# A hybrid pool/SSD layer: the transposed copies of x and B come from VectorE blocks and a trip through DRAM

## The chip, the cores and the metric

The kernel runs on one core of a Trainium2 chip. The metric is the device time of one execution in microseconds (us). Three executions were timed. One further execution was profiled; every row below is from it.

## What is computed

One layer of a streaming encoder on 384 tokens (256 of a prompt, 8 streams with 16 tokens each), model width 2048, everything in float32. The part that matters here is branch B, a Mamba-2 scan with 8 groups of 8 heads:

```python
proj = u @ w_in                       # columns: pool | z | xBC | dt | gates
xbc  = silu(causal_conv(proj[xBC]))   # x: 4096 columns, B: 1024, C: 1024
# per chunk and group g, heads r of the group:
cb  = einsum('btgn,bsgn->btsg', C, B)
xdt = x * dt
y   = einsum('btgr,bsgrp->btgrp', cb * decay, xdt) + einsum('btgn,bgrpn->btgrp', C, h) * exp(cum)
h   = h * exp(last) + einsum('bsgn,bsgr,bsgrp->bgrpn', B, w_end, xdt)
```

A projection leaves its columns (channels) on the partitions and the tokens along the row. The products with `xdt`, and those that make the new state out of B and x, need the tokens on the partitions. So of each group four tiles of x and one tile of B, each 128 channels x 384 tokens, are wanted transposed as well: 40 tiles in all.

## The kernel before

**Matmuls.** Weights and activations are split into a high and a low part in fp32r (`wsplit`, lines 66-72: ScalarE copies the high part, VectorE subtracts to get the low one), and each product is three matmuls (`mm3`, lines 97-100). A projection (`proj`, line 126) is two halves (`half`, line 106) of 8 x 3 matmuls; each half uses one weight tile of 512 KB, fetched by a DMA issued from the SP queue (`wfetch`, line 61). There are three buffers for fetched tiles and three for each split part. `take` (line 117) keeps three weight tiles in preparation: it issues the fetch and the split of the tile two halves ahead before the half itself.

**The scan stage** (lines 549-933) goes through 8 groups. A group projects 10 column tiles, that is 20 halves: B, C, x0, x1, x2, x3, then z0 to z3. After each x, B or C projection `conv_in` and `taps` (lines 565-593) evict it, run the convolution on VectorE and ScalarE and end with the SiLU that writes the tile `xs`.

Between projections stand short runs of small matmuls, called lumps here. One lies in the middle of the group, after x2's projection, and one at its end. The lump in the middle serves the second pair of heads of the group before and the first pair of this group; the one at the end serves the first and the second pair of this group. A lump holds, in this order, `t_pp` (new prompt state), `t_trx` (the transpositions of a pair's two x tiles on TensorE, three 128x128 blocks each, into PSUM), in the middle lump also `t_cb` (C times B) and `t_trB` (the transposition of B), then `t_yT`, `t_Y`, `t_yi`, and `t_su` (state of the streams).

`xside` (line 716) multiplies the transposed x out of PSUM by two per-token factors into `xdt` and `xdw`, splits `xdw` into `xhl`, and sends the last 128 tokens of it to DRAM and back in another order (`x_scr`, then 8 loads into `xst`). `bside` (line 688) splits the transposed B into `Bhl` and does the same (`b_scr`, then 8 loads into `bst`). `xhl` and `Bhl` go into `t_pp`, `xst` and `bst` into `t_su`, `xdt` into `t_Y`.

**Order.** A planner orders each engine's instructions, and the SP queue's DMAs, by program order and by when its own model says that they can start. TensorE is tied further: `chain` and `last` put each half and each lump behind the one before. An engine, and the SP queue, then works strictly in that order: what waits holds up what stands behind it.

Of the kernel before, what the change touches and what calls it, by code (L numbers as in the profile page):

```python
# [14 lines left out]
P = 128  # L15
# [18 lines left out]
def build(ctx, tc, io):  # L34
# [82 lines left out]
    def take(src, name):  # L117
# [5 lines left out]
        assert got == name, (got, name)  # L123
        return hl

    def proj(units, rhs, name):
        o = bank[0](f"pj_{name}")[:, :T]
        for q, src in enumerate(units):
            half(o, q, take(src, f"{name}_{q}"), rhs)
        return o  # L130

    def moving(o, units, lhs, tail, done, pool=None, own=0, hook=None, mid=None):
# [65 lines left out]
    gb_scr = [dram.tile([P, 3, 512], F32, name=f"gb_scr{i}") for i in range(4)]  # L198
    b_scr = [dram.tile([P, 2, P], F32, name=f"b_scr{i}") for i in range(G)]
    x_scr = [dram.tile([P, 2, 2, P], F32, name=f"x_scr{i}") for i in range(16)]  # L200
    cum_scr = dram.tile([NH, T], F32, name="cum_scr")
    dec_scr = dram.tile([NH, NB], F32, name="dec_scr")

# [345 lines left out]
    with tc.tile_pool(name="phd", bufs=2, reuse_waits="tile") as pd, tc.tile_pool(  # L549
# [45 lines left out]
        def conv(ui, c, tag, nb):  # L595
            return taps(conv_in(ui, c), c, tag, nb)

        def lump(fn):
            with behind(last[0]):
                last[0] = fn()  # L600
# [12 lines left out]
                sy.dma_start(cbc, cum_scr[S.h0 + q * 2 : S.h0 + q * 2 + 2, :].partition_broadcast(P))  # L613
                S.cbcs.append(cbc)

        def t_trB(D):
            D.tr = sstile(f"trB{D.g}")
            for b in range(3):
                i = te.transpose(D.tr[:, b * P : b * P + P], D.BT[:, b * P : b * P + P], ident)
            return i  # L620

        def t_cb(D):
            D.cb = sstile(f"cb{D.g}")
            for sb, t0, c0, n in ((0, 0, 0, 256), (1, P, 256, P), (2, TP, T, P)):
                i = te.matmul(
                    D.cb[:, c0 : c0 + n], D.BT[:, sb * P : sb * P + P], D.CT[:, t0 : t0 + n], start=True, stop=True
                )
            return i

        def t_trx(S):  # L630
            S.trs = []
            for j in S.js:
                tr = sstile(f"trx{S.g}_{j}")
                for b in range(3):
                    i = te.transpose(tr[:, b * P : b * P + P], S.D.xs[j][:, b * P : b * P + P], ident)
                S.trs.append(tr[:, :T].rearrange("p (b h q) -> p b h q", b=3, h=2))
            return i

        def t_yi(S):
# [46 lines left out]
            return i  # L686

        def bside(D):
            D.Bhl = pd.tile([P, 2, 3, P], F32R, tag="Bhl", name=f"Bhl{D.g}")
# [4 lines left out]
            sy.dma_start(bscr, D.Bhl[:, :, 2, :].bitcast(F32))  # L694
            D.bs = bst[D.g % 2]
            for p4 in range(4):
                for h2 in range(2):
                    sy.dma_start(
                        D.bs[h2 * 64 + p4 * 16 : h2 * 64 + p4 * 16 + 16].bitcast(F32),
                        bscr.rearrange("(q h r) l n -> h l r q n", q=4, h=2)[h2, p4 // 2],  # L700
                    )

        def cside(D):
            D.Cm = pd.tile([P, 2, P], F32, tag="Cm", name=f"Cm{D.g}", bufs=1)
# [10 lines left out]

        def xside(S):
            S.xdt = pd.tile([P, 2, 3, P], F32, tag="xdt", name=f"xdt{S.nm}")
            S.xdw = pd.tile([P, 2, 3, P], F32, tag="xdw", name=f"xdw{S.nm}", bufs=1)
# [15 lines left out]
            S.xhl = pd.tile([P, 2, 2, 3, P], F32R, tag="xhl", name=f"xhl{S.nm}", bufs=1)  # L734
            s.activation(S.xhl[:, 0], S.xdw, AF.Copy)
            v.tensor_tensor(S.xhl[:, 1], S.xdw, S.xhl[:, 0].bitcast(F32), ALU.subtract)
            xscr = x_scr[S.qd]
            for l in range(2):
                sy.dma_start(xscr[:, l], S.xhl[:, l, :, 2, :].bitcast(F32))
            S.xst = pd.tile([P, 4, 2 * P], F32R, tag="xst", name=f"xst{S.nm}", bufs=1)  # L740
            for p4 in range(4):
                for h2 in range(2):
                    sy.dma_start(
                        S.xst[h2 * 64 + p4 * 16 : h2 * 64 + p4 * 16 + 16].bitcast(F32),
                        xscr.rearrange("(q h r) l j n -> h l r q (j n)", q=4, h=2)[h2, p4 % 2],
                    )

        def eside(S, q):
            if q == 0:
# [99 lines left out]
        for g in range(G + 1):  # L849
            if g == G:  # L850
                eside(prev.p[1], 0)
                eside(prev.p[1], 1)
                dside(prev.p[1])
                gate_b(0, pd, "hs")
                py = mmtile("pp_last")
                lump(lambda: t_pp(prev.p[1], py))
                lump(lambda: t_yT(prev.p[1]))
                lump(lambda: t_Y(prev.p[1]))
                state(prev.p[1])
                final(prev.p[1])  # L860
# [8 lines left out]
            D.BT = conv(u0, 32 + g, "BT", 2)  # L869
            pload(D.p[0])  # L870
            if g:
                eside(prev.p[1], 0)
            D.CT = conv(u0 + 1, 40 + g, "CT", 2)
            if g:
                eside(prev.p[1], 1)
            D.xs.append(conv(u0 + 2, g * 4, "xs", 6))
            if g:
                dside(prev.p[1])
            cload(D.p[0])
            cside(D)  # L880
            D.xs.append(conv(u0 + 3, g * 4 + 1, "xs", 6))
# [48 lines left out]
            state(S)  # L930
            final(S)
            prev = D
# [519 lines left out]
```

## Time and profile before

| | |
|---|---|
| median of 3 executions | 2655.25 us (2655.15 to 2655.45) |
| profiled execution, its own time | 2655.5 us |
| span of its instructions | 2653.7 us |
| TensorE (PE) busy | 2641.6 us |
| VectorE (DVE) busy | 1507.7 us |
| ScalarE (ACT) busy | 1168.8 us |
| the 8 groups of the scan stage | from about 419 to 1131 us of the span |
| one group | about 90 us |

How to read the rows: PE is TensorE's matmuls and PEld its weight loads, SPq the queue of the DMAs that SyncE issues, L70 is line 70 of the kernel, and `wh_x<-w_x` is a tile written and the tile read. "x8" counts instructions. A row of a timeline or of the chain begins with its start and its duration in us, and in brackets stands how long the engine was idle before it and what ended that. A row of the waits tells who waited for whom, us in total, how often, and the longest. Matmuls are pipelined, so the time from one start to the next is what counts.

### The profile page before, as it was taken

To read this page: it belongs to the slowest core of one execution; us is meant where nothing else is said; L and a number is where in the kernel's file an instruction comes from. 1 tells how busy PE (TensorE), PEld (TensorE's weight loads), DVE (VectorE), ACT (ScalarE), POOL (GpSimd) and SP (SyncE) were. 2 spreads that over 40 slices of the span, in tenths; PEclk is the share of its full clock that TensorE was granted. 3 is DMA by queue.
4 is the path that set the end of the run, shared out by engine and by line. 5 is a ranking of instruction groups with operands and counts; after the bars stand their busy time and mean duration, and the time that the engine had idled before them with its cause. 6 is when DMAs were issued, how large, how long until landed. Compare 5 with 4: busy or idle time off the path is not lost.

```text
span 2653.7 us, 38432 instructions
## 1 busy us (share of the span) xinstructions
PE 2641.6 (100%) x15269; PEld 2462.2 (93%) x15269; DVE 1507.7 (57%) x2108; ACT 1168.8 (44%) x1820; POOL 134.5 (5%) x166
## 2 busy tenths in 40 slices
PE   9999999999999999999999999999999999999998
PEld 8998889999999999988888889999999999989897
DVE  6585335788787879856343336534444444444446
ACT  6443225557575756545322235433333333333233
POOL 0000000011111111120000000000000000000000
PEclk9999999999999999999999999999999999999999
DMA  7444445556666666657444543433333343334433
GB/s 273 153 133 156 147 147 205 199 200 218 210 230 210 213 211 223 221 201 254 171 151 163 188 160 132 143 135 135 135 135 135 135 137 135 136 135 135 138 136 129
DMA packets 146163, 451.35 MB, mean 170 GB/s; under 512 B 17920, under 2 KB 45120, under 8 KB 140992
## 3 DMA queue, kind: packets, MB, share of 16 engines
q1 hardware_dynamic: 134400, 389.90, 43.0%
q0 software_dynamic: 11584, 59.00, 6.0%
q8 instruction: 120, 1.97, 0.3%
q14 instruction: 59, 0.48, 0.1%
HBM read 407.11 MB, written 41.72 MB: 169 GB/s over the span
## 4 chain that ended last, share of the span: by engine, by line
PE 97%; ACT 1%; DVE 1%; DMA 1%; issue 0%; SPq 0%; DVEq 0%; ACTq 0%
PE pj_up L98 6%; PE pj_up L100 6%; PE pj_up L99 6%; PE wd L143 6%; PE wd L142 6%; PE wd L141 6%; PE pj_x L98 4%; PE pj_x L99 4%; PE pj_x L100 4%; PE pj_z L100 3%; PE pj_z L99 3%; PE pj_z L98 3%; PE pj_sp L142 3%; PE pj_sp L141 3%; PE pj_sp L143 3%; PE pj_gb L141 2%
## 5 line engine op out<-in xcount | busy, mean ns | idle before, releaser
L98 PE MATMUL pj_up<-x1h,wh_up 128*128 128x384 f32 (+1 forms) x1024 | 333.7, 326 | 0.0
L99 PE MATMUL pj_up<-x1l,wh_up 128*128 128x384 f32 (+1 forms) x1024 | 333.4, 326 | 0.0
L100 PE MATMUL pj_up<-x1h,wl_up 128*128 128x384 f32 (+1 forms) x1024 | 333.4, 326 | 0.0
L71 DVE TENSOR_TENSOR wl_wd<-w_wd,wh_wd 128x1024 fp32r<-128x1024 f32 x126 | 154.3, 1225 | 240.8 <-ACT wh_wd L70 240.8
L141 PE MATMUL wd<-wh_wd,hh 128*128 128x512 f32 x756 | 286.5, 379 | 0.0
L142 PE MATMUL wd<-wl_wd,hh 128*128 128x512 f32 x756 | 286.5, 379 | 0.0
L143 PE MATMUL wd<-wh_wd,hl 128*128 128x512 f32 x756 | 286.5, 379 | 0.0
L70 ACT ACTIVATE wh_wd<-w_wd 128x1024 fp32r<-128x1024 f32 x126 | 133.1, 1057 | 322.6 <-PE wd L143 262.1
L70 ACT ACTIVATE wh_up<-w_up 128x1024 fp32r<-128x1024 f32 x126 | 133.1, 1056 | 292.0 <-PE pj_up L99 231.8
L71 DVE TENSOR_TENSOR wl_up<-w_up,wh_up 128x1024 fp32r<-128x1024 f32 x126 | 154.3, 1225 | 178.1 <-ACT wh_up L70 178.0
L98 PE MATMUL pj_x<-xgh,wh_x 128*128 128x384 f32 x768 | 251.9, 328 | 0.1
L100 PE MATMUL pj_x<-xgh,wl_x 128*128 128x384 f32 x768 | 250.4, 326 | 0.0
L99 PE MATMUL pj_x<-xgl,wh_x 128*128 128x384 f32 x768 | 250.4, 326 | 0.0
L99 PEld LDWEIGHTS pj_up<-x1l,wh_up 128*128 128x128 f32 x1024 | 193.6, 189 | 0.2
L98 PEld LDWEIGHTS pj_up<-x1h,wh_up 128*128 128x128 f32 x1024 | 193.6, 189 | 0.2
L100 PEld LDWEIGHTS pj_up<-x1h,wl_up 128*128 128x128 f32 x1024 | 193.6, 189 | 0.0
L98 PE MATMUL pj_z<-xgh,wh_z 128*128 128x384 f32 x512 | 166.9, 326 | 0.0
L99 PE MATMUL pj_z<-xgl,wh_z 128*128 128x384 f32 x512 | 166.9, 326 | 0.0
L100 PE MATMUL pj_z<-xgh,wl_z 128*128 128x384 f32 x512 | 166.9, 326 | 0.0
L71 DVE TENSOR_TENSOR wl_sp<-w_sp,wh_sp 128x1024 fp32r<-128x1024 f32 x64 | 78.4, 1224 | 154.0 <-ACT wh_sp L70 154.0
L143 PEld LDWEIGHTS wd<-wh_wd,hl 128*128 128x128 f32 x756 | 142.9, 189 | 20.3
L142 PEld LDWEIGHTS wd<-wl_wd,hh 128*128 128x128 f32 x756 | 142.9, 189 | 20.1
(333 smaller groups left out, 5880.6 us busy)
## 6 DMA issues: line engine op xcount, KB each, us to landing
w_up<-w_up SPq DMA_DIRECT2D x128, 512.0 KB, 3.2
w_wd<-w_down SPq DMA_DIRECT2D x128, 512.0 KB, 3.2
w_x<-w_in SPq DMA_DIRECT2D x96, 512.0 KB, 3.6
w_z<-w_in SPq DMA_DIRECT2D x64, 512.0 KB, 3.4
w_sp<-w_ssd SPq DMA_DIRECT2D x64, 512.0 KB, 3.2
w_ga<-w_ga SPq DMA_DIRECT2D x32, 512.0 KB, 3.2
w_pp<-w_pp SPq DMA_DIRECT2D x32, 512.0 KB, 3.2
hs<-ssm POOLq DMA_DIRECT2D x16, 1024.0 KB, 7.0
```

Of the source, the lines that this page charges most:

```text
L70: cut[0] = s.activation(h, w, AF.Copy)
L71: cut[1] = v.tensor_tensor(l, w, h.bitcast(F32), ALU.subtract)
L98: te.matmul(out, wh, xh, start=first, stop=False, **how)
L99: te.matmul(out, wh, xl, start=False, stop=False, **how)
L100: return te.matmul(out, wl, xh, start=False, stop=last, **how)
L141: te.matmul(out, mh, vh, start=k == 0, stop=False)
L142: te.matmul(out, mh, vl, start=False, stop=False)
L143: last[0] = te.matmul(out, ml, vh, start=False, stop=k == nk - 1)
```

## The change

- The 96 transpositions of x (`t_trx`) and the 24 of B (`t_trB`) on TensorE are gone.
- In their place each of the 40 tiles takes a trip, `turned`: VectorE transposes it in 32x32 blocks (`v.transpose`, 128x384, SBUF to SBUF); four DMAs, one for 32 partitions each, write the blocks to their places in a DRAM tile `t_scr` in runs of 32 elements (128 bytes, 384 runs per DMA); one DMA reads it back in rows of 512 bytes with the tokens on the partitions.
- The trip's steps (`turn`, `spread`, read) are put on a list; `tick`, after each half of a projection, lets every listed trip go one step. The old DMA trips of `bside` and `xside` (out, and back) are put on the same list instead of being issued on the spot.
- The projections of a group go x0, x1, B, C, x2, x3 in place of B, C, x0, x1, x2, x3; the columns of the weights follow.
- `xdw` is no tile of its own any more: the second product is written over the transposed x, `xT`. The block-transposed tile `xb` shares its two buffers with the convolution's accumulator, `cacc`.
- In the last group, where no projection follows, `gate_b` calls `tick` at two of its weight tiles.

```diff
+    def tick():
+        for todo in steps:
+            todo.pop(0)()
+        steps[:] = [todo for todo in steps if todo]
     def proj(units, rhs, name):
         for q, src in enumerate(units):
             half(o, q, take(src, f"{name}_{q}"), rhs)
+            tick()
...
+    t_scr = [dram.tile([T, P], F32, name=f"t_scr{i}") for i in range(40)]
...
+        def turned(src, i, o):
+            xb, scr = [], t_scr[i]
+            def turn():
+                xb.append(pd.tile([P, T], F32, tag="cacc", name=f"xb{i}"))
+                v.transpose(xb[0], src)
+            def spread():
+                for q in range(4):
+                    p32 = slice(q * 32, q * 32 + 32)
+                    sy.dma_start(
+                        scr[:, p32].rearrange("(j a) b -> a j b", a=32),
+                        xb[0][p32].rearrange("p (j b) -> p j b", b=32),
+                    )
+            steps.append([turn, spread, lambda: sy.dma_start(o, scr.rearrange("(b t) n -> t b n", b=3))])
+        def xturned(D, g, j):
+            S = D.p[j // 2]
+            if j % 2 == 0:
+                S.xT = pd.tile([P, 2, 3, P], F32, tag="xT", name=f"xT{S.nm}", bufs=1)
+            turned(D.xs[j], g * 4 + j, S.xT[:, j % 2])
...
-        def t_trB(D):
-            D.tr = sstile(f"trB{D.g}")
-            for b in range(3):
-                i = te.transpose(D.tr[:, b * P : b * P + P], D.BT[:, b * P : b * P + P], ident)
...
-        def t_trx(S):
-            for j in S.js:
-                tr = sstile(f"trx{S.g}_{j}")
-                for b in range(3):
-                    i = te.transpose(tr[:, b * P : b * P + P], S.D.xs[j][:, b * P : b * P + P], ident)
...
         def bside(D):
-            s.activation(bh, D.tr[:, :T], AF.Copy)
-            v.tensor_tensor(bl, D.tr[:, :T], bh.bitcast(F32), ALU.subtract)
+            s.activation(bh, bl.bitcast(F32), AF.Copy)
+            v.tensor_tensor(bl, bl.bitcast(F32), bh.bitcast(F32), ALU.subtract)
...
+            steps.append([lambda: sy.dma_start(bscr, D.Bhl[:, :, 2, :].bitcast(F32)), back])
...
         def xside(S):
-            for q, tv in enumerate(S.trs):
-                for o, i in ((S.xdt, 3), (S.xdw, 6)):
+            for q in range(2):
+                tv = S.xT[:, q].rearrange("p b (h q) -> p b h q", h=2)
+                for o, i in ((S.xdt, 3), (S.xT, 6)):
...
-            s.activation(S.xhl[:, 0], S.xdw, AF.Copy)
+            s.activation(S.xhl[:, 0], S.xT, AF.Copy)
...
+            steps.append([out, back])
...
-            cs = [32 + g, 40 + g] + [g * 4 + j for j in range(4)]
+            cs = [g * 4, g * 4 + 1, 32 + g, 40 + g, g * 4 + 2, g * 4 + 3]
...
-                gate_b(0, pd, "hs")
+                gate_b(0, pd, "hs", {0: tick, 2: tick})
...
-            lump(lambda: t_trx(S))
             lump(lambda: t_cb(D))
-            lump(lambda: t_trB(D))
...
             D.xs.append(taps(b2, g * 4 + 2, "xs", 6))
+            xturned(D, g, 2)
             D.xs.append(conv(u0 + 5, g * 4 + 3, "xs", 6))
+            xturned(D, g, 3)
...
-            lump(lambda: t_trx(S1))
```

More of the change, by code (lines that the diff above doesn't have):

```diff
@@ L124, in take @@
         return hl
+    steps = []
+    def tick():
+        for todo in steps:
+            todo.pop(0)()
+        steps[:] = [todo for todo in steps if todo]
     def proj(units, rhs, name):
@@ L614, in cload @@
                 S.cbcs.append(cbc)
-        def t_trB(D):
-            D.tr = sstile(f"trB{D.g}")
-            for b in range(3):
-                i = te.transpose(D.tr[:, b * P : b * P + P], D.BT[:, b * P : b * P + P], ident)
-            return i
         def t_cb(D):
@@ L627, in t_cb @@
                 )
-            return i
-        def t_trx(S):
-            S.trs = []
-            for j in S.js:
-                tr = sstile(f"trx{S.g}_{j}")
-                for b in range(3):
-                    i = te.transpose(tr[:, b * P : b * P + P], S.D.xs[j][:, b * P : b * P + P], ident)
-                S.trs.append(tr[:, :T].rearrange("p (b h q) -> p b h q", b=3, h=2))
             return i
@@ L688, in bside, with back @@
         def bside(D):
-            D.Bhl = pd.tile([P, 2, 3, P], F32R, tag="Bhl", name=f"Bhl{D.g}")
             bh, bl = (D.Bhl[:, a].rearrange("p b n -> p (b n)") for a in range(2))
-            s.activation(bh, D.tr[:, :T], AF.Copy)
-            v.tensor_tensor(bl, D.tr[:, :T], bh.bitcast(F32), ALU.subtract)
+            s.activation(bh, bl.bitcast(F32), AF.Copy)
+            v.tensor_tensor(bl, bl.bitcast(F32), bh.bitcast(F32), ALU.subtract)
             bscr = b_scr[D.g]
-            sy.dma_start(bscr, D.Bhl[:, :, 2, :].bitcast(F32))
             D.bs = bst[D.g % 2]
[L696 to L701, printed above, removed]
+            def back():
+                for p4 in range(4):
+                    for h2 in range(2):
+                        sy.dma_start(
+                            D.bs[h2 * 64 + p4 * 16 : h2 * 64 + p4 * 16 + 16].bitcast(F32),
+                            bscr.rearrange("(q h r) l n -> h l r q n", q=4, h=2)[h2, p4 // 2],
+                        )
+            steps.append([lambda: sy.dma_start(bscr, D.Bhl[:, :, 2, :].bitcast(F32)), back])
         def cside(D):
@@ L717, in xside @@
             S.xdt = pd.tile([P, 2, 3, P], F32, tag="xdt", name=f"xdt{S.nm}")
-            S.xdw = pd.tile([P, 2, 3, P], F32, tag="xdw", name=f"xdw{S.nm}", bufs=1)
-            for q, tv in enumerate(S.trs):
-                for o, i in ((S.xdt, 3), (S.xdw, 6)):
+            for q in range(2):
+                tv = S.xT[:, q].rearrange("p b (h q) -> p b h q", h=2)
+                for o, i in ((S.xdt, 3), (S.xT, 6)):
                     v.tensor_tensor(
@@ L734, in xside, with out, back @@
             S.xhl = pd.tile([P, 2, 2, 3, P], F32R, tag="xhl", name=f"xhl{S.nm}", bufs=1)
-            s.activation(S.xhl[:, 0], S.xdw, AF.Copy)
-            v.tensor_tensor(S.xhl[:, 1], S.xdw, S.xhl[:, 0].bitcast(F32), ALU.subtract)
+            s.activation(S.xhl[:, 0], S.xT, AF.Copy)
+            v.tensor_tensor(S.xhl[:, 1], S.xT, S.xhl[:, 0].bitcast(F32), ALU.subtract)
             xscr = x_scr[S.qd]
[L738 to L746, printed above, removed]
+            def out():
+                for l in range(2):
+                    sy.dma_start(xscr[:, l], S.xhl[:, l, :, 2, :].bitcast(F32))
+            def back():
+                S.xst = pd.tile([P, 4, 2 * P], F32R, tag="xst", name=f"xst{S.nm}", bufs=1)
+                for p4 in range(4):
+                    for h2 in range(2):
+                        sy.dma_start(
+                            S.xst[h2 * 64 + p4 * 16 : h2 * 64 + p4 * 16 + 16].bitcast(F32),
+                            xscr.rearrange("(q h r) l j n -> h l r q (j n)", q=4, h=2)[h2, p4 % 2],
+                        )
+            steps.append([out, back])
         def eside(S, q):
@@ L868, in build @@
             D.xs, D.zs = [], []
-            D.BT = conv(u0, 32 + g, "BT", 2)
+            D.Bhl = pd.tile([P, 2, 3, P], F32R, tag="Bhl", name=f"Bhl{g}")
+            D.xs.append(conv(u0, g * 4, "xs", 6))
+            xturned(D, g, 0)
             pload(D.p[0])
@@ L872, in build @@
                 eside(prev.p[1], 0)
-            D.CT = conv(u0 + 1, 40 + g, "CT", 2)
+            D.xs.append(conv(u0 + 1, g * 4 + 1, "xs", 6))
+            xturned(D, g, 1)
             if g:
                 eside(prev.p[1], 1)
-            D.xs.append(conv(u0 + 2, g * 4, "xs", 6))
+            D.BT = conv(u0 + 2, 32 + g, "BT", 2)
+            turned(D.BT, 32 + g, D.Bhl[:, 1].bitcast(F32))
             if g:
@@ L879, in build @@
             cload(D.p[0])
+            D.CT = conv(u0 + 3, 40 + g, "CT", 2)
             cside(D)
-            D.xs.append(conv(u0 + 3, g * 4 + 1, "xs", 6))
             b2 = conv_in(u0 + 4, g * 4 + 2)
@@ L1377 @@
     for g in range(G):
+        cols += [6144 + (g * 4 + j) * P for j in range(2)]
         cols += [6144 + 4096 + g * P, 6144 + 5120 + g * P]
-        cols += [6144 + (g * 4 + j) * P for j in range(4)]
+        cols += [6144 + (g * 4 + j) * P for j in range(2, 4)]
         cols += [2048 + (g * 4 + j) * P for j in range(4)]
```

## The prediction

> **What bounds the kernel now.** First the page: TensorE's busy time, and the engines on the chain that ended last.
>
> ```profile
> PE 2641.6 (100%) x15269; PEld 2462.2 (93%) x15269; DVE 1507.7 (57%) x2108; ACT 1168.8 (44%) x1820; POOL 134.5 (5%) x166
> PE 97%; ACT 1%; DVE 1%; DMA 1%; issue 0%; SPq 0%; DVEq 0%; ACTq 0%
> ```
>
> TensorE works all the time, so what leaves its queue leaves the time, if nothing makes it wait. Next, who TensorE waited for over the whole span (us in total, times, longest):
>
> ```profile
> PE warm_o L229 <- DVE warm L225: 1.2, 1, 1.2
> PE trx L635 <- ACT xs L592: 0.6, 1, 0.6
> ```
>
> The scan stage has one wait, 0.6 us in its first group. Last, the stretches: one group of 90 us.
>
> ```profile
> core 0: us, PE busy (x) PEld busy (x) DVE busy (x) ACT busy (x) POOL busy (x), PEclk, DMA share, GB/s
> 681.00:771.00 90.00, 90.00 (x667) 87.66 (x666) 74.73 (x108) 57.40 (x111) 13.02 (x13) 1.00 0.63 216
> ```
>
> TensorE is full, VectorE idles 15.3 us of 90 and the DMA engines 37%. The kernel's averages mislead here: VectorE's 57% is 83% in this stage, and this is the only stage that the change touches.
>
> **The change, part by part.**
>
> *Transpositions leave TensorE.* The chain in the middle lump of one group, then the counts over the span by tile:
>
> ```profile
> 635.71 0.66 PE trx L635 x6
> 636.36 0.88 PE cb L625 x6
> 637.24 0.33 PE trB L619 x3
> ```
>
> ```profile
> L635 PE MATMUL trx<-cst,xs x96: 272/273/328, 457.9 to 1131.0; 128*128 128x128 f32 x96
> ```
>
> ```profile
> L619 PE MATMUL trB<-cst,xs x24: 272/273/273, 460.2 to 1086.5; 128*128 128x128 f32 x24
> ```
>
> One transposition holds TensorE for 0.66/6 = 0.11 us (its 273 ns are pipelined over the next ones). 96/6 x 0.66 + 24/3 x 0.33 = 10.6 + 2.6 = 13.2 us, all of it on the path, or 1.65 us per group. The 0.6 us of the first group stay: `t_cb`, now first in that lump, waits for C's SiLU instead, since C is the fourth projection as x1 was.
>
> *Block transpositions come to VectorE.* The trace has none. Rows of its forms in one group:
>
> ```profile
> L815 DVE TENSOR_TENSOR zs<-zs,xs 128x384 f32<-128x384 f32 x4 | 2.1, 546 | 0.0
> L765 DVE TENSOR_TENSOR E<-E,cbm 128x1024 f32<-128x1024 f32 x4 | 5.1, 1284 | 0.0
> L174 DVE TENSOR_SCALAR ny_g<-ssum 128x384 int32<-128x384 int32 x1 | 0.4, 352 | 0.0
> ```
>
> Ends: 0.35 us (as many elements, one operand) and 1.28 us (far more elements). I take 0.55, the row of the same shape from SBUF to SBUF: 5 x 0.55 = 2.8 us per group, hidden in 15.3 us of idleness. `xside` and `bside` keep their counts and shapes and only read SBUF instead of PSUM: nothing. [...]
>
> *Trips come to the DMA engines.* A tile's trip is 4 x 384 = 1536 runs of 128 bytes and 384 of 512. The trace has no run of 128 bytes. A stretch of 3.8 us with nearly nothing but 512-byte runs, then a stretch of 900 us with 4 KB ones:
>
> ```profile
> q1 hardware_dynamic: 700, 0.31, 28.9%
> ```
>
> ```profile
> q1 hardware_dynamic: 33284, 121.15, 39.3%
> ```
>
> 0.289 x 16 x 3.8 us / 700 = 25 ns each; 0.393 x 16 x 900 / 33284 = 170 ns. So a 128-byte run costs at least nothing and at most 170 ns; I take 25, since 512 bytes is nearest. Per trip (1536 + 384) x 25 / 16 = 3.0 us, per group 15 us: the share goes from 0.63 to 0.80. Free are 0.37 x 90 = 33 us, reads take 3; 30 x 16 us / 7680 = 63 ns is the price from which the DMA engines bound the stage. [...]
>
> *Issues come to the SP queue.* Issue times and waits of SP (the waits over the seven groups from 501 to 1131 us):
>
> ```profile
> L743 SPq DMA_DIRECT2D xst<-x_scr x128: 302/424/1647, 470.0 to 1143.9; - x128
> ```
>
> ```profile
> SPq L63 <- DVE wl_x L71: 210.6, 74, 4.3
> SPq L63 <- DVE wl_z L71: 94.7, 42, 3.8
> ...
> SPq L739 <- ACT xhl L735: 22.3, 14, 2.4
> ...
> SPq L743 <- DMA x_scr<-xhl: 12.1, 15, 2.9
> ```
>
> 25 issues more per group at 0.42 = 10.5 us; SP sits (210.6 + 94.7)/7 = 44 us per group waiting for a free weight buffer. The planner places SP's DMAs by its own model, so two new waits can be in the wrong place: `spread` for the block transposition, the read for the four writes to land. Where the planner put such a DMA too early, it blocked SP by 22.3/14 = 1.6 us and 12.1/15 = 0.8 us. Weight fetches stand behind, and then splits and TensorE. A landing takes some 2 us:
>
> ```profile
> b_scr<-Bhl SPq DMA_DIRECT2D x8, 128.0 KB, 2.1
> ```
>
> How late may a fetch be? The tight place, behind the middle lump of one group, by queue (SP, ACT, DVE, PE):
>
> ```profile
> 742.74 0.60 SPq L743 DMA_DIRECT2D xst<-x_scr  x1
> 743.44 4.10 SPq L63 DMA_DIRECT2D w_z<-w_in  x3
> ```
>
> ```profile
> 749.78 1.04 ACT L70 ACTIVATE wh_z<-w_z 128x1024 fp32r<-128x1024 f32 x1
> ```
>
> ```profile
> 737.31 1.21 DVE L71 TENSOR_TENSOR wl_z<-w_z,wh_z 128x1024 fp32r<-128x1024 f32 x1
> ...
> 743.66 1.21 DVE L71 TENSOR_TENSOR wl_z<-w_z,wh_z 128x1024 fp32r<-128x1024 f32 x1
> ...
> 750.85 2.36 DVE L71 TENSOR_TENSOR wl_z<-w_z,wh_z 128x1024 fp32r<-128x1024 f32 x2 [1.07 <-ACT wh_z L70]
> ```
>
> ```profile
> 746.68 0.33 PE L98 MATMUL pj_z<-xgh,wh_z 128*128 128x384 f32 x1
> ```
>
> ```profile
> 754.80 0.33 PE L98 MATMUL pj_z<-xgh,wh_z 128*128 128x384 f32 x1
> ```
>
> The buffer came free at 738.5 (end of the split at 737.31), but SP was still issuing the loads of `xst`, so the fetch started at 743.4, 4.9 us late. Its split ended at 750.85 + 1.2 = 752.1, and the half that uses it (counted along the queue) began at 754.8: 2.7 us to spare. Two halves before, the split ended at 744.9 and TensorE came at 746.7: 1.8 us, VectorE being late there.
>
> *What becomes earlier.* `xdt`, the second product and `Bhl` no longer wait for TensorE's lump, but for a read that landed before. In the lump VectorE loses 4 x 0.55 + 0.55 = 2.7 us to an earlier, idle time, just ahead of the 1.8 us spot. `xhl` still waits for `t_pp`, which reads its only buffer, and that stands first in the lump. So `x_scr`, `xst`, `b_scr` and `bst` (2 + 8 + 1 + 8 issues) can be sent earlier than now, though listed one and two half projections later; their reader `t_su` is in the next lump, some 40 us off. They go past SP's weight fetches only; POOL's queue is untouched.
>
> *The margin of a trip.* The slowest to be wanted is B's: its projection is the third, its reader `bside` stands behind the fifth. From a projection's eviction to its SiLU, on VectorE and ScalarE:
>
> ```profile
> 627.28 0.62 DVE L572 TENSOR_TENSOR cbuf<-pj_x,rstd 128x192 f32<-128x192 f32 x2 [0.96 <-PE pj_x L100]
> ```
>
> ```profile
> 631.30 0.61 ACT L592 ACTIVATE xs<-cacc,vec 128x384 f32<-128x384 f32 x1 [0.39 <-DVE cacc L588]
> ```
>
> 4.6 us; with 0.55, 4 x 0.42, 2.1, 0.42 and 2.1 the trip ends 11.5 us behind the projection. A half is 8 x 0.49 = 3.9 us (three matmuls in 0.49):
>
> ```profile
> 746.19 0.33 PE L98 MATMUL pj_z<-xgh,wh_z 128*128 128x384 f32 x1
> ```
>
> Four halves are 15.6 us, so 4 us remain. If they are gone, ScalarE waits in `bside`, with weight splits behind it.
>
> `xb` shares two buffers with `cacc`, so the transposition of the next tile must wait until the spread of the one before has landed. That is 4.6 + 0.55 + 1.7 + 2.1 = 9.0 us behind the earlier projection; the next transposition can start 7.8 + 4.6 = 12.4 us behind it. The 3.4 us between are what SP may be late before VectorE, too, waits with weight splits queued behind it. I cost this wait at nothing, on the strength of that margin.
>
> In the last group two ticks inside `gate_b` send the last pair's 2 + 8 DMAs; their reader stands behind all of `gate_b`, eight weight tiles later: nothing.
>
> *The first group* has less to spare than the others: ScalarE runs late there, and this split ended just as TensorE began the half that uses it.
>
> ```profile
> 448.69 1.23 DVE L71 TENSOR_TENSOR wl_x<-w_x,wh_x 128x1024 fp32r<-128x1024 f32 x1 [1.80 <-ACT wh_x L70]
> ```
>
> ```profile
> 450.06 0.33 PE L98 MATMUL pj_x<-xgh,wh_x 128*128 128x384 f32 x1
> ```
>
> 449.92 against 450.06, 0.14 us. A block transposition of 0.55 us ahead of it makes TensorE wait 0.4 us, once.
>
> Sum against the profiled execution: 2655.5 - 13.2 + 0.4 = 2642.7 us. That execution lies 0.25 above the median of the runs, so 2642.5 is what the median should become.
>
> **The rivals.**
>
> *SP late (slower).* In each group one trip goes ahead of the fetch at the tight place and blocks it: five issues 2.1, landing 2.1, planner's error 1.6, together 5.8 us against 2.7 to spare. 8 x (5.8 - 2.7) = 25, less 13.2: 2667. Two such places per group would make 2692. For it: SP was 4.9 us late there already. Against: VectorE's and SP's work there moves ahead, and elsewhere SP waits for buffers. It turns the gain into a loss from 2.7 + 1.65 = 4.4 us of blocking at one place per group.
>
> *Dear 128-byte writes (slower).* Above 63 ns the stage is DMA-bound. At 75 ns a group needs 0.63 x 90 + 3 + 7680 x 0.075/16 = 95.7 us in place of 90: 8 x 5.7 = 46, so 2701; the 13.2 us on TensorE are worth nothing then. At the far end, 170 ns, it would be 0.63 x 90 + 3 + 81.6 = 141 us per group and 3065. For it: nothing like it was measured. Against: 512 bytes cost 25.
>
> *Splits late (half the gain).* Block transpositions or late trips push weight splits past the 1.8 us, 0.8 us of wait per group: 2642 + 6.4 = 2649.
>
> *No measurable change.* The same with 1.6 us per group: TensorE's saved time returns as its waits for splits, 2655. That asks for VectorE or ScalarE to be the real limit; 15.3 and 32.6 us idle per group speak against it.
>
> **How the numbers follow.** A measurement tells 0.2%, 5.3 us, from no change: 2649.9 to 2660.6. Full gain (2640.5 to 2646): 0.62; half the gain: 0.07; none: 0.09; SP late: 0.14; dear writes: 0.05; other slowdowns, such as a planner's order that sets splits too late: 0.03. Faster 0.69, same 0.09, slower 0.22. The likeliest case alone spans 2640.5 to 2646; the range goes on to the SP case, up to 2668, and leaves out the dear writes and what lies below.
>
> **What would show it.** Right: the middle lump shorter by 1.0 us and the end lump by 0.66, no PE wait but the first group's; block transpositions near 0.55 us; DMA share about 0.8 or less; spreads that land in 2 to 3 us. Wrong: PE waits for `wl_x` or `wl_z`, with SP's `w` fetches waiting behind spreads or reads; ScalarE idle before `Bhl`; a DMA share near 1.

## The result, and the profile after

The changed kernel takes 2698.0 us (median of 5 runs, 2695.27 to 2704.45) against 2655.25 us before: ratio 1.016, 95% interval 1.0149 to 1.0172. It is 43 us slower, where 13 us faster was forecast. The profiled execution took 2695.27 us, its span 2693.5 us.

From the page of the changed kernel, the engines' busy time; the 120 transpositions are gone from TensorE (15149 instructions in place of 15269), and TensorE is no longer busy all the time. (A matmul that runs at a lower granted clock counts as busy for longer: 0.53 us at 543.85 us, in the first stretch of half clock shown below, in place of 0.33.)

```profile
PE 2648.2 (98%) x15149; PEld 2455.2 (91%) x15149; DVE 1535.4 (57%) x2148; ACT 1171.6 (43%) x1820; POOL 108.9 (4%) x166
```

Who TensorE waited for (us in total, times, longest). The kernel before has one such wait in the scan stage, of 0.6 us.

```profile
PE pj_z L98 <- ACT wh_z L70: 13.7, 13, 1.8
PE pj_z L100 <- DVE wl_z L71: 9.9, 14, 1.2
PE pj_x L100 <- DVE wl_x L71: 5.5, 8, 0.9
PE pj_x L98 <- ACT wh_x L70: 2.6, 3, 1.0
PE cb L651 <- ACT xs L601: 2.1, 1, 2.1
```

39 waits with 33.8 us in all, nearly all of them for weight splits. The waits of the SP queue over the same seven groups as in the prediction (501 to 1131 us) say why the splits are late. SP's waits for a free weight buffer, the cover on which the forecast rested, have fallen from 210.6 + 94.7 to 132.0 + 32.8 us, and in their place it waits for the transposed block, 28 times, 88.2/28 = 3.2 us each. L617 is the spread.

```profile
SPq L63 <- DVE wl_x L71: 132.0, 45, 5.9
SPq L617 <- DVE xb L612: 88.2, 28, 4.7
SPq L63 <- DVE wl_z L71: 32.8, 18, 3.5
```

One such place, just ahead of the middle lump of a group, in the timeline (start, length, engine; in brackets the idle time before and what ended it):

```profile
523.19 1.23 DVE L71 TENSOR_TENSOR wl_x<-w_x,wh_x 128x1024 fp32r<-128x1024 f32 x1 [0.64 <-ACT wh_x L70]
...
525.73 1.86 SPq L617 DMA_DIRECT2D t_scr<-xb  x4
...
527.63 0.47 SPq L645 DMA_DIRECT2D cbc<-cum_scr  x1
...
529.86 0.58 DVE L612 STREAM_TRANSPOSE xb<-xs 128x384 f32<-128x384 f32 x1 [0.69 <-ACT xs L601]
530.47 0.30 SPq L617 DMA_DIRECT2D t_scr<-xb  x1
...
530.95 0.38 SPq L622 DMA_DIRECT2D xT<-t_scr  x1
531.39 2.09 SPq L617 DMA_DIRECT2D t_scr<-xb  x3
...
533.52 0.47 SPq L645 DMA_DIRECT2D cbc<-cum_scr  x1
534.03 0.43 SPq L63 DMA_DIRECT2D w_x<-w_in  x1
...
540.39 1.06 ACT L70 ACTIVATE wh_x<-w_x 128x1024 fp32r<-128x1024 f32 x1 [3.15 <-PE pj_x L99]
...
541.50 0.43 PE L98 MATMUL pj_x<-xgh,wh_x 128*128 128x384 f32 x1 [1.01 <-ACT wh_x L70]
```

The weight buffer came free at 523.19 + 1.23 = 524.4. SP first sent the spread of x0, then stood from 528.1 to 530.47 in front of the spread of x1, whose block VectorE transposed only at 529.86. The fetch went out at 534.03, 9.6 us late, and landed at 540.3. ScalarE had been idle for 3.15 us until then (its bracket names a matmul that ended at the same instant) and TensorE waited for ScalarE at 541.50. In the kernel before, the split of the same half had 5.4 us to spare (in the group that the prediction shows it ended at 711.5, and the half began at 716.9). The second place is behind the middle lump, the tight place of the prediction. Of the 39 waits 37 stand at three of a group's 20 halves alone, the ninth (this place) and the 16th and 17th (the second place), and each time the fetch had gone out 6 to 13 us after its buffer came free. In the kernel before only the fetch for the 17th half is late, by 4.2 us (median of seven groups).

Two things make such a wait dearer than its idle time. First the restart: from the matmul before (540.17) to the one at 541.50 lie 1.33 us, of which 1.01 are shown as idle and 0.16 are the usual distance; the next one starts another 0.27 later in place of 0.16. If each of the 39 waits costs these 0.27 us, that makes 10 us. Second the granted clock. In stretches of 3.4 us (the columns after the length are busy time of PE, PEld, DVE, ACT and POOL with counts, the granted clock, the DMA share and GB/s), the first stretch stands right behind two waits, the second follows it:

```profile
543.85:547.25 3.40, 3.40 (x12) 3.40 (x12) 2.40 (x5) 0.89 (x3) 0.00 (x0) 0.50 0.92 290
547.50:550.90 3.40, 3.40 (x23) 3.40 (x22) 2.19 (x4) 3.02 (x5) 0.00 (x0) 1.00 0.11 42
```

At half the clock TensorE does 12 matmuls in the time of 23. The stage has five such stretches, each a loss of 1.7 us, 8.5 us together. So by this estimate 33.8 + 10 + 8.5 = 52 us are lost and 13.2 won, 39 us net; the two profiled executions differ by 2695.27 - 2655.5 = 39.8.

### The profile page after: what moved, and what is told of

It is laid out like the page before. It is cut to its first block, busy times and chain, and to the rows that moved or that the text cites. A ratio compares the mean times of both kernels' runs of the same rounds, so it can differ in the third digit from the quotient of the medians.

```text
span 2693.5 us, 38584 instructions
## 1 busy us (share of the span) xinstructions
PE 2648.2 (98%) x15149; PEld 2455.2 (91%) x15149; DVE 1535.4 (57%) x2148; ACT 1171.6 (43%) x1820; POOL 108.9 (4%) x166
## 4 chain that ended last, share of the span: by engine, by line
PE 57%; DVE 1%; DMA 1%; ACT 0%; SPq 0%; issue 0%; DVEq 0%; ACTq 0%
PE pj_up L98 6%; PE pj_up L99 6%; PE pj_up L100 6%; PE wd L151 6%; PE wd L149 6%; PE wd L150 6%; PE pj_sp L149 3%; PE pj_sp L151 3%; PE pj_sp L150 3%; PE pj_gb L149 2%; PE pj_gb L150 2%; PE wo L150 2%; PE wo L149 2%; PE pj_gb L151 2%; PE wo L151 2%; PE pj_z L100 0%
## 5 line engine op out<-in xcount | busy, mean ns | idle before, releaser
L149 PEld LDWEIGHTS wd<-wh_wd,hh 128*128 128x128 f32 x756 | 142.9, 189 | 20.1
```

The source lines that it names most:

```text
L149: te.matmul(out, mh, vh, start=k == 0, stop=False)
```

## The experiments

Four theories stood against each other. Theory 1, which I held after the trace: weight fetches come late because the SP queue, which works in order, holds them behind DMAs of the trips that wait or are being issued. Theory 2: the 128-byte runs slow all transfers. Theory 3: VectorE, in order too, waits for reads to land, with weight splits behind it. Theory 4: the new order and the stepping of the old trips cost the time by themselves. Each ratio is to the kernel before on the same chip, with its 95% interval.

**Order and steps alone.** From the kernel before, with the PE transpositions kept:

```diff
-            cs = [32 + g, 40 + g] + [g * 4 + j for j in range(4)]
+            cs = [g * 4, g * 4 + 1, 32 + g, 40 + g, g * 4 + 2, g * 4 + 3]
...
+            steps.append([out, back])
```

> The kernel before with one part of the change: the projections in the new order and the old trips of B and of xhl advanced one step per half projection; the transpositions stay on TensorE. Theory 1 (the weight fetches of the SP queue stand behind the new trips), theory 2 (the 128-byte runs slow all landings) and theory 3 (VectorE waits for reads to land): none of their causes is here, so about the time of before, 2650 to 2660 us, and TensorE never waits for a weight split for more than some 3 us in all. Theory 4 (the new order and the stepping of the old trips cost the time by themselves): most of the 43 us of the whole change, 2685 to 2700 us.

2656.39 us, 0.9999 (0.9989 to 1.0008). Theory 4 falls. TensorE's one wait in the scan stage:

```profile
PE pj_x L98 <- DVE cbuf L580: 0.3, 1, 0.3
```

**The waits alone.** To that kernel are added the block transpositions and spreads with almost nothing in them:

```diff
+                    sy.dma_start(scr[:32, p32], xb[0][p32, :32])
...
+            steps.append([turn, spread])
```

> The kernel with the new order and the stepped old trips and nothing else of the change (2656 us), plus the block transpositions and spreads that carry almost nothing: each of the four DMAs of a spread writes 32 runs of 128 bytes in place of 384, nothing is read back, and TensorE keeps its transpositions. So the SP queue waits for the transposed blocks and sends four DMAs per tile, but there is no traffic to speak of and VectorE waits for no read. Theory 1 (weight fetches behind DMAs of the SP queue that wait): spreads wait for the block some 3 us each, fetches behind them are late at the same two places, TensorE waits for splits for 15 us or more, 2670 to 2710 us. Theory 2 (traffic) and theory 3 (VectorE waits for reads): 2654 to 2660 us, no waits.

2698.48 us, 1.016 (1.0143 to 1.0177): 43 us lost, without the traffic, without a read, and with the transpositions still on TensorE. The changed kernel, from which the transpositions are gone, loses these 43 us and the 13 us that they should have brought, 56 in all; so this run has some three quarters of its loss. First the stage from 422 to 1167 us (DMA share 0.61; 0.62 in the kernel before), then TensorE's largest wait, then the place behind the middle lump in the timeline:

```profile
422.00:1167.00 745.00, 719.30 (x5099) 694.89 (x5098) 584.50 (x850) 448.97 (x848) 92.30 (x96) 0.98 0.61 203
```

```profile
PE pj_z L98 <- ACT wh_z L70: 18.5, 8, 2.7
```

```profile
561.27 5.51 SPq L772 DMA_DIRECT2D xst<-x_scr  x8
568.31 8.74 SPq L617 DMA_DIRECT2D t_scr<-xb  x8
577.14 1.33 SPq L63 DMA_DIRECT2D w_z<-w_in  x3
...
581.20 1.06 ACT L70 ACTIVATE wh_z<-w_z 128x1024 fp32r<-128x1024 f32 x1 [6.27 <-DMA w_z<-w_in]
```

Behind the loads of `xst`, which end at 566.8, stand the eight spreads of x2 and x3; they are through at 577.1, so the first fetch, whose buffer was free at 563.1, goes out 10.3 us later for them. ScalarE waits 6.27 us for the weights, TensorE 2.75 us for ScalarE. So waits and issues of the SP queue are enough for 43 us. That is theory 1; theories 2 and 3 are not needed for them. Nearly all of it comes from the place behind the middle lump: ahead of the lump fetches are late here too, by 8.4 us, but TensorE waits there no more than 0.6 us in a group, while in the changed kernel it waits 8.1 us in all for splits of x. The other 13 us of the changed kernel follow late fetches as well, by its own trace (above); how much the traffic adds there to the lateness, this run does not show.

**Long runs.** Spreads write rows of 1536 bytes; the placing of the blocks is left out:

```diff
-                        scr[:, p32].rearrange("(j a) b -> a j b", a=32),
-                        xb[0][p32].rearrange("p (j b) -> p j b", b=32),
+                        scr.rearrange("(p x) n -> p (x n)", x=3)[p32],
+                        xb[0][p32],
```

> The changed kernel with the spreads writing whole rows of 1536 bytes (32 runs per DMA in place of 384 of 128 bytes); the same issues, waits, steps and bytes. The placing of the blocks is left out, so the transposed copies are wrong. Theory 2 (128-byte runs slow the landings): the whole loss goes, 2640 to 2655 us. Theory 1: the waits of SP for the transposition stay, only the landings of the spreads get shorter, 2685 to 2700 us. Theory 3: reads can go and land about 1 us earlier, 2680 to 2700 us. Theory 4: 2690 to 2700 us.

2677.82 us, 1.008 (1.0065 to 1.0095), outside of every range: 20 of the 43 us come back. The stalls ahead of the middle lump are gone, those behind it stay. The weights of x land no sooner (median 4.3 us against 4.2), those of z do (3.9 against 4.6). The planner sets another order for DMAs of another shape, so this run does not price the short runs by themselves; the mended kernel below shows what they cost where the fetches have room.

**A late spread.** An empty step ahead of the spread, so that one more fetch is listed before it:

```diff
-            steps.append([turn, spread, lambda: sy.dma_start(o, scr.rearrange("(b t) n -> t b n", b=3))])
+            steps.append([turn, lambda: None, spread, lambda: sy.dma_start(o, scr.rearrange("(b t) n -> t b n", b=3))])
```

> The changed kernel with an empty step between the block transposition and the spread, so the spread is listed one half projection later and the read with it. Theory 1: the spread no longer waits for VectorE in the SP queue, so the waits of spreads for the transposed block fall from 100 us to under 30 us, and the time to 2650 to 2680 us. Theory 2: the same transfers, 2690 to 2700 us. Theory 3: reads land 4 us later still, VectorE waits longer for them, 2700 to 2720 us. Theory 4: 2690 to 2700 us.

2667.68 us, 1.0036 (1.0022 to 1.0051): 30 of the 43 us come back, as theory 1 has it, though by less waiting than expected, since the spreads' waits fell only from 100 to 81 us. It seems to count more which fetch stands behind them. VectorE's waits for reads fell as well, from 24.8 to 8.3 us, where theory 3 had them grow, so this run alone does not part theory 1 from theory 3. The place ahead of the middle lump is gone; what TensorE still waits for in every group is the one behind it:

```profile
PE pj_z L98 <- ACT wh_z L70: 9.1, 8, 2.5
PE pj_z L100 <- DVE wl_z L71: 5.3, 8, 0.7
```

**Late spread and long runs together** (the edits of both).

> The changed kernel with the empty step ahead of the spread and spreads in rows of 1536 bytes; the placing of the blocks is left out, so the transposed copies are wrong. If the two causes are separate and add up (31 us and 21 us alone): the whole loss and the 13.2 us come back, 2640 to 2650 us. If both only shorten the same blocking of the SP queue at the place behind the middle lump, and the one behind x2 and x3 remains: 2655 to 2668 us.

2672.95 us, 1.0065 (1.005 to 1.008): the two do not add up, and the time lies above both ranges. The wait behind the middle lump stays, and, as with the long runs alone, the order of VectorE brings one of up to 0.8 us for `cbm`.

**Other queues.** The spreads and reads on POOL's queue (`gp.dma_start`), and in a second kernel the spreads alone on ScalarE's (`s.dma_start`):

> The changed kernel with the five DMAs of each new trip (four spreads, one read) issued on POOL's queue in place of SP's; the same instructions, bytes, runs and steps otherwise. Theory 1 (the weight fetches stand behind waiting trip DMAs in the SP queue): the waits for weight splits go, 2640 to 2655 us. Theory 2 (the 128-byte runs slow all landings): nothing changes for the transfers, 2690 to 2700 us. Theory 3 (VectorE waits for reads to land): the same reads, so 2685 to 2705 us. Theory 4 (order and stepping): 2690 to 2700 us.

> The changed kernel with the four spreads of each trip issued on ScalarE's queue in place of SP's; the read stays on SP, all runs and bytes stay. Theory 1: SP no longer waits for the transposed block (100 us of waits gone) nor issues the spreads, so fetches are late only behind the reads; against that, 5 x 4 issues per group and the wait for the block now lie on ScalarE, with the weight splits behind them, some 8 us of 33 us idle per group: 2645 to 2675 us. Theory 2: the same transfers, 2690 to 2700 us. Theory 3: 2680 to 2700 us.

2698.98 us, 1.0159 (1.0143 to 1.0174), and 2703.09 us, 1.0181 (1.0164 to 1.0198). Both miss what theory 1 gave (the first lies in the ranges of the three others, the second above all), and the waits show why: the blocking moved. On POOL the spreads wait up to 13.5 us, the reads come late, and VectorE waits for them, so that here theory 3's wait is real:

```profile
POOL t_scr L617 <- DVE xb L612: 156.3, 35, 13.5
```

```profile
DVE xdt L740 <- DMA xT<-t_scr: 64.2, 19, 6.5
```

With the spreads on ScalarE's queue, the reads on SP wait for the spreads to land (8.4 us in all in the changed kernel), with the fetches behind them:

```profile
SPq L622 <- DMA t_scr<-xb: 189.1, 63, 9.1
```

**A fourth weight buffer.** Each fetch is listed one half projection earlier; one buffer each is taken from B, C and xs:

```diff
+        if extra[0] is not None and name[0] in "xz" and nfetch[0] % 4 == 0:
+            w = extra[0].tile([P, 1024], F32, tag="w4", name=f"w_{name}")
...
+        while queue and len(got_) < (1 if len(ready) >= 3 else 2):
+            got_.append((queue[0][1], wfetch(*queue.pop(0))))
```

> The changed kernel with a fourth buffer for fetched weight tiles in the scan stage, so that each fetch is listed one half projection (3.9 us) earlier; the trips, their queue, their runs and their waits stay. The room comes from single buffers for B and C in place of two and five for xs in place of six. Theory 1 (weight fetches come late, because the SP queue holds them behind the trips): the lateness of 5 to 13 us at two places per group loses 3.9 us, so TensorE's waits for splits shrink to under 10 us and the time goes to 2645 to 2670 us, while the waits of the spreads for the transposed block stay near 100 us. Theory 2 (128-byte runs slow the transfers): landings stay at 4.2 to 4.6 us or grow, a part comes back all the same, 2670 to 2690 us. Theory 3 (VectorE waits for reads, with splits behind it): the waits for xT stay near 25 us, 2680 to 2700 us.

2711.27 us, 1.0209 (1.0194 to 1.0224), outside of all three. Both old places are gone, and one wait of 6.2 us per group has come, elsewhere. In VectorE's order (timeline of one group) the weight split now stands behind the chain of the norm, whose first instruction waited for TensorE:

```profile
678.00 0.56 DVE L211 TENSOR_SCALAR ssum<-bc_g 128x384 f32<-128x384 f32 x1 [3.66 <-PE bc_g L209]
...
685.02 2.20 DVE L866 SCALAR_TENSOR_TENSOR zs<-zs,vec,ny_g 128x384 f32<-128x384 f32 x4
687.14 1.21 DVE L77 TENSOR_TENSOR wl_z<-w_z,wh_z 128x1024 fp32r<-128x1024 f32 x1
```

**Fourth buffer and late spread together.**

> The changed kernel with both the fourth buffer for fetched weight tiles and the empty step ahead of the spread. Theory 1: no fetch is late by more than the new margin, TensorE waits for almost no split, and the 13.2 us of the transpositions show: 2640 to 2648 us. Theory 2: the 128-byte runs still slow the landings, 2655 to 2675 us. Theory 3: 2665 to 2700 us.

2679.06 us, 1.0088 (1.0073 to 1.0103). Theory 1 missed again. The time is in theory 3's range, but VectorE waits only 7.8 us for reads; TensorE waits at the norm's chain alone, 1.5 and 2.0 us per group, and once 5.4 us in the first group, where the new buffer's space was not free yet.

**Those two mended.** The norm's chain is ordered behind the split listed before it, and the fourth buffer starts with the second group:

```diff
-        v.tensor_scalar(halves(hm), even_odd(o), -0.5 / n, -0.5 * EPS, ALU.mult, ALU.add)
+        with later() if name[0] == "g" else nullcontext():
+            v.tensor_scalar(halves(hm), even_odd(o), -0.5 / n, -0.5 * EPS, ALU.mult, ALU.add)
...
+        if extra[0] is not None and name[0] in "xz" and nfetch[0] > 20 and nfetch[0] % 4 == 0:
```

> The kernel with four weight buffers and the late spread, and two things mended: the first instruction of the norm's chain on VectorE is ordered behind the weight split that is listed before it, and the fourth buffer is used from the second group on. The order of the SP queue stays. Its waits were 1.5 + 2.0 us per group at the norm's chain, and 5.4 us once in the first group. If those two were all that was left: 2640 to 2650 us. If the fetches are late all the same, or the split's place in VectorE's order moves the wait elsewhere: 2660 to 2680 us.

2644.24 us (2643.79 to 2644.48), 0.9953 (0.9937 to 0.997): 12.7 us below the 2656.93 of the kernel before in these runs, and faster than both kernels. The stretch of 90 us that the prediction quoted, then TensorE's waits in the stage, then SP's:

```profile
681.00:771.00 90.00, 90.00 (x672) 87.14 (x664) 79.17 (x117) 57.96 (x113) 9.84 (x13) 1.00 0.78 240
```

```profile
PE pj_x L106 <- DVE wl_x L77: 0.9, 1, 0.9
...
PE pj_x L104 <- ACT wh_x L76: 0.4, 1, 0.4
```

```profile
SPq L631 <- DVE xb L626: 79.0, 31, 4.6
```

All 128-byte runs are still there, the DMA engines are busier in this stretch (0.78) than in the kernel before (0.63) and in the changed one (0.68), the weights of x land later than in the changed kernel (median 4.8 us against 4.2; those of z 4.6 in both), and spreads still wait 79 us: with room for the fetches none of it costs TensorE anything. So here the short runs cost nothing by themselves: 12.7 us came of the 12.8 that were forecast. What slower landings added in the changed kernel, where the fetches had no such room, is not shown.

**The mends without the change.** Fourth buffer and norm's chain, in the kernel before:

> The kernel before with the fourth weight buffer (from the second group on), single buffers for B and C, five for xs, and the norm's chain behind the split; no trips, the transpositions on TensorE. If the gain of the mended kernel (about 2644 us) comes from the transpositions that left TensorE: nothing here, 2650 to 2658 us, since TensorE waits for nothing in the scan stage of the kernel before. If the mends are a gain by themselves: 2640 to 2650 us.

2656.9 us, 1.0001 (0.9992 to 1.001). So the 12.7 us are the transpositions that left TensorE.

**The mends without the late spread.**

> The mended kernel without the empty step ahead of the spread: the changed kernel with the fourth weight buffer from the second group on and the norm's chain behind the split. With the fourth buffer, and without the other mends, TensorE waited 6.2 us per group at the norm's chain and 5.2 us in the first group, nowhere else. If the margin of the fetch alone pays for the waits of the SP queue: 2642 to 2650 us, with the waits of the spreads for the transposed block back at 100 us or more. If the spread must be late as well: 2655 to 2690 us.

2667.84 us, 1.0047 (1.0033 to 1.0061). The fourth buffer and the tie, without the step of delay, bring 30 us, not all; the spreads wait 115 us. Of TensorE's waits that remain, 5.8 us are for splits and 10.5 us for other work of VectorE, 4.7 of these for `cbm`. VectorE in turn waits for reads, so a part of the rest may be theory 3:

```profile
DVE xdt L754 <- DMA xT<-t_scr: 34.7, 22, 3.1
```

In the mended kernel with the late spread this wait is 7.2 us. That a later spread makes VectorE wait less for its read goes against theory 3; the order on VectorE changes with it, and which of its moves does it was not tried.

**Old trips drawn out,** with the late spread, and in a second kernel all mends together:

```diff
+            steps.append([rest] + out + [rest] + [lambda i=i: back([i]) for i in range(4)])
```

> The kernel with the late spread, and behind the middle lump the old trips drawn out as well: one empty step ahead of the writes to b_scr and x_scr and one behind them, and the 8 + 8 loads of bst and xst two by two over four steps in place of all at once. Same DMAs, same bytes. Theory 1 (what is left of the loss lies at the one place behind the middle lump, where the SP queue sends 19 DMAs of the old trips and the spreads of x2 ahead of the fetch of the sixteenth weight tile): TensorE's waits of about 1.5 us per group there go, 2645 to 2658 us. If that place is late for another reason (landings among the 128-byte runs): 2662 to 2672 us.

> All of it together: four weight buffers, late spread, old trips drawn out, the norm's chain behind the split. If the loss is nothing but places where the order of SP's or VectorE's queue puts waiting work ahead of weight fetches and splits: no wait of TensorE for a split is left and the 13.2 us of the transpositions show, 2640 to 2646 us, faster than both kernels. If the 128-byte runs or the added work on VectorE cost by themselves: 2655 us or more.

2685.0 us, 1.0104 (1.0089 to 1.0119), and 2663.42 us, 1.0026 (1.0016 to 1.0036): both slower than without this edit. The first is outside of both ranges; the second is in the range of the costly runs, which the mended kernel, with the same runs and work at 2644.24, rules out. In the first, TensorE waits for the low part of a split, 20.5 us in seven places, and in five of these not at all for the high part:

```profile
PE pj_z L100 <- DVE wl_z L71: 20.5, 7, 4.5
```

```profile
580.80 1.07 ACT L70 ACTIVATE wh_z<-w_z 128x1024 fp32r<-128x1024 f32 x1 [5.48 <-DMA w_z<-w_in]
```

```profile
574.67 0.55 DVE L199 TENSOR_SCALAR ssum<-bc_g 128x384 f32<-128x384 f32 x1
...
580.99 2.21 DVE L861 SCALAR_TENSOR_TENSOR zs<-zs,vec,ny_g 128x384 f32<-128x384 f32 x4
583.11 0.55 DVE L744 TENSOR_TENSOR xdt<-xT,tok 128x384 f32<-128x384 f32 x1
583.58 1.22 DVE L71 TENSOR_TENSOR wl_z<-w_z,wh_z 128x1024 fp32r<-128x1024 f32 x1
```

At the place that the edit aimed at, the 16th and 17th half of a group, no wait is left; the seven stand at the 19th half. Its fetch is 8 to 10 us late there (ScalarE waited 5.48 us for the weights), and VectorE is late too: the high part was ready at 581.87, but VectorE, without an idle moment, came to the low part only at 583.58, behind the norm's chain and the four products that follow it. In the second kernel the high part lies ready for 5 to 6.5 us, and TensorE waits 9.4 us in five places for the low part behind that chain. SP's wait for `xhl` ahead of `x_scr` is no sign of the loss: it is 81.1 us in the first kernel, 63.5 with the late spread alone, and 57.8 in the mended kernel. So drawing out the trips cleared one place and, by the planner's new order, made another.

## Why the prediction was wrong, point by point

- **Transpositions off TensorE, 13.2 us: right.** The middle lumps follow each other at 726.20 - 636.36 = 89.8 us before and at 88.2 us in the mended kernel; forecast were 1.65 us less. The mended kernel's 12.7 us against the 12.8 of the sum say the same.
- **Block transposition, 0.55 us taken: right.** Mean 576 ns:

```profile
L612 DVE STREAM_TRANSPOSE xb<-xs 128x384 f32<-128x384 f32 x40 | 23.0, 576 | 25.7 <-ACT xs L601 25.7
```

 That `xside` and `bside` read SBUF in place of PSUM cost next to nothing, as taken: `xdt` 559 ns (median) against 548 before, `Bhl` on VectorE 550 against 545. Not foreseen: VectorE stood 25.7 us at the head of its queue waiting for the SiLU.
- **128-byte runs, 25 ns taken: twice too dear, and the rival of dear writes is out.** The trace has a record of each run. In the changed kernel from 422 to 1167 us the 61440 runs of 128 bytes took 12.5 ns on average, the 29184 of 512 bytes 27.8 ns. A group's trips are then 5 x (1536 x 12.5 + 384 x 27.8)/16 = 9.3 us of the DMA engines in place of 15. In the stretch of 90 us the share rose from 0.63 to 0.78 in the mended kernel, forecast 0.80; that it came so near is in part luck, since other runs took longer beside the trips (those of 4 KB 194 ns in the changed kernel, 187 before, both from 422 to 1167 us) and its groups are 2% shorter.
- **SP queue: this step failed.** Its issues were counted rightly (0.47 us each, 0.42 taken), but the planner's error of 1.6 us was taken from `x_scr` behind `xhl` and set against the 44 us per group that SP sat waiting for a free weight buffer. A spread waits for its block 3.2 us, four times per group, and an average of idle time is no cover at the two places where a fetch is due. At the tight place that the prediction named, with 2.7 us to spare, the spreads of x2 and x3 take 10.3 us in the waits-alone run, and the loads of `xst`, which "can be sent earlier than now", still stand right ahead of them. The rival "SP late" had the mechanism, and its case of two places per group, 2692, came near the 2698.0. Its chance was too small because the trips' waits were set into SP's idle time on average. That the number came so near is in part luck: it counts 16 x 3.1 = 50 us of idle time alone, where the trace has 33.8 us of it and some 18 us of what follows a wait. The place ahead of the lump was not looked at: its 5.4 us to spare were more than at the tight place, and its fetch was 9.6 us late.
- **What becomes earlier: failed.** `xdt` was to find its read landed; VectorE waited for it 24.8 us in all, 19 times:

```profile
L740 DVE TENSOR_TENSOR xdt<-xT,tok 128x384 f32<-128x384 f32 x32 | 17.8, 557 | 25.1 <-DMA xT<-t_scr 24.8
```

- **The margin of B's trip: right.** ScalarE shows no wait for `Bhl` in the changed kernel. Nor does VectorE or ScalarE wait for a spread to land, to reuse the buffers that `xb` and `cacc` share; the prediction cost that wait at nothing.
- **First group, 0.4 us: too small.** TensorE waited 0.7 us for a split and 2.1 us for the SiLU ahead of `t_cb`; before it was 0.6 us.
- **The price of a wait: mis-sized.** The rivals counted idle time alone. Restart and half clock added about 18 us to 33.8, by the estimate above.

## What to carry to other kernels

In a queue that works in order, as SP's does here (behind spreads that waited, the fetch at 534.03 us of the changed kernel went out 9.6 us late), a new DMA must be priced by what stands behind it at the moment it waits, place by place; here the idle time of the queue on average covered nothing. When work is taken off the engine that bounds the kernel, check the lead of the prefetch that feeds it: here one more buffer, a step of delay and one tie in VectorE's order turned 1.6% slower into 0.5% faster, while the buffer alone, the step alone, and the buffer with either of the other two did not. A planner that orders by its own model lays the whole stage anew after each edit, so look for the new place before judging the edit.

## What the runs showed of the hardware

In the scan stage of the changed kernel TensorE's granted clock fell to 0.50 five times, for 3.41 us each, at waits of which the longest took 1.01 to 2.07 us. One of the five followed a single wait of 2.07 us (first the row of the wait, then the stretch behind it, with the clock at 0.50):

```profile
461.82 0.76 PE L651 MATMUL cb<-xs,xs 128*128 128x256 f32 x1 [2.07 <-ACT xs L601]
```

```profile
461.90:465.30 3.40, 3.40 (x22) 2.15 (x22) 2.98 (x6) 2.32 (x5) 0.00 (x0) 0.50 1.06 378
```

In the kernel with the late spread a wait of 2.10 us at the same place was not followed by it (the two rows below), and neither was a wait of 2.02 us in the kernel with four buffers and the late spread (clock 1.00 from 593.30 to 596.60 us, behind the matmul that ended the wait at 593.26):

```profile
461.77 0.48 PE L651 MATMUL cb<-xs,xs 128*128 128x256 f32 x1 [2.10 <-ACT xs L601]
```

```profile
461.90:465.30 3.40, 3.05 (x28) 2.32 (x29) 2.94 (x6) 2.28 (x5) 0.00 (x0) 1.00 1.06 369
```

Nor is one long wait needed: the half clock at 543.85 in the changed kernel followed waits of 1.01 and 0.67 us. One group later waits of 0.98 and 0.67 us were not followed by it:

```profile
640.00:643.40 3.40, 3.40 (x23) 3.40 (x22) 2.40 (x5) 0.90 (x3) 0.00 (x0) 1.00 0.80 244
```

So in these runs the length of a wait alone does not decide. In the trace of the changed kernel the stretches from one change of the clock to the next are whole multiples of 3.41 us long (the first four of the scan stage 1, 23, 1 and 39 times); whether it matters where a wait falls in that raster was not tried.
